# Second layer norm of a one-layer decoder: the last two experts' first-block rows become norm blocks of their own

## The chip, the cores and the metric

The kernel runs on one core of a Trainium2 chip. The metric is device time in microseconds (us) of one execution; less is better. Before the change the median of three runs is 1563.72 us (1562.43 to 1565.71). The engines are PE (TensorE, matmuls), DVE (VectorE), ACT (ScalarE), POOL (GpSimd) and SP (SyncE, which here only issues DMAs). Each engine works through its own instructions in order.

## The reference, cut to what matters

```python
def reference(x, ...):                                  # 1024 tokens, width 1024, one layer
    mix = hybrid_mixer(x, ...)                          # attention and DeltaNet branches, merged, times w_o
    x = layer_norm(ALPHA * x + mix, ln1_g, ln1_b)
    ffn = grouped_moe(x, w_router, router_bias, w_gate, w_up, w_down)
    return layer_norm(ALPHA * x + ffn, ln2_g, ln2_b)

merged = sigmoid(g_a) * (o_a @ w_br_a) + sigmoid(g_b) * (o_b @ w_br_b)     # end of hybrid_mixer
mix = merged @ w_o

# grouped_moe: each token goes to its two best experts (of 16) of one group of four
hid = silu(xb @ w_gate[e]) * (xb @ w_up[e])
ys = (hid @ w_down[e]) * row_w                          # summed per token over its two experts
```

All arrays are float32.

## The kernel before, in words

A value is split into a high and a low float32r part: ACT copies the high part (`copy`), DVE subtracts it for the low part (`lo_part`), and each product is three matmuls (`mm3`: high by high, high by low, low by high). So every weight that PE uses has passed through ACT and then DVE.

Working tiles are taken from a pool `m4` of 45 slots of 128 x 1024 (names m and l in the rows) and `m2` of 128 x 512 (h). A small model of the engines (`Clock`) only decides which free slot is taken; it puts the order of instructions in place in the first part of the kernel, and the parts that matter here are written out by hand, after `tc.manual_schedule()`. Waits between engines and DMAs follow from the tiles.

Two places of the program matter.

*Merging the branches* (`merge(d)`, eight steps, d = 0 to 7; products in tiles `pbr`). A step takes branch weights (`w_br_a`, `w_br_b`) that were split in the step before, makes four products of twelve matmuls each, and DVE multiplies each by a gate `sg`. At its start it issues on SP the loads that the next steps need: two gates (`spill`), branch weights for step d + 2, and one slab of `w_o`. In its middle it splits the branch weights of step d + 1 and the `w_o` slab; at its end ACT makes the next two gates (Sigmoid). On ACT the order over a step's border is thus: high part of the `w_o` slab of step 0, the two gates of step 1, the high part of the branch weights of step 2. DVE makes the low parts in program order between the multiplications. Right ahead of the first step, `route_consts` clears the buffers of the routing: it fills a zero tile `z` and issues on SP two stores of it (to the spare rows of `h_d` and `acc_d`) and two of initial lists (`lst`).

*Experts and second norm.* `acc_d` in HBM holds ALPHA * x per token; every expert block adds its rows by an indirect DMA (`acc_d<-m,idx`). The first block of an expert (up to 128 tokens) runs in `expert_steps` (16 steps j: eight for gate and up, products `pgu`; eight for down, `pdn`); further blocks of an expert run before it in conditional branches. The first block of expert 15 does not add its rows to `acc_d`: it gathers its rows into `lt[0]`, adds its own result, norms them as a block of their own and scatters them to the output after all others. The other rows are loaded from `acc_d` in eight blocks (`more_rows`) and normed by the generator `norm_rows`, whose pieces are put between the steps of expert 15 by the table `TAIL` (the count of pieces at each j). Per block ACT sums (Copy with accumulation) and squares (Square with accumulation), DVE forms mean, variance and two passes over the block (SCALAR_TENSOR_TENSOR), POOL takes the power -1/2 (TENSOR_TENSOR `h<-rs,mhalf`), and SP stores the block.

Of the kernel before, what the change touches and what calls it, by code (L numbers as in the profile page):

```python
# [169 lines left out]
HIGHS = 8  # L170
START = 'LLLLABHUHNLUHLUHLLUSRCLIDLLUL'
LASTF = (1, 2, 1, 0, 2, 0, 1, 0, 1, 1, 1, 1, 1, 0, 0, 0)
TAIL = (0, 0, 0, 1, 1, 0, 1, 0, 1, 0, 1, 0, 1, 1, 1, 1)
TR0 = 5
TR = 2
TURN = (2, 3, 4, 5)
# [13 lines left out]
def build(ctx, tc, x, w_in, conv_w, a_log, dt_bias, onorm_g, w_br_a, w_br_b, w_o, ln1_g, ln1_b,  # L190
# [802 lines left out]
    lst = [dp.tile([NE * S, 2], FT, name=f"lst{j}") for j in range(2)]  # L993
    h_d = dp.tile([S + JUNK, D], FT, name="h_d")
    acc_d = dp.tile([S + JUNK, D], FT, name="acc_d")
    BIG = 1.0e30
    wr = kp.tile([P, KT, NE], FT, name="wr_")
    rc = kp.tile([P, 3, NE], FT, name="rc")
# [13 lines left out]
    def route_consts():  # L1012
        Q.dma_start(wr, w_router.rearrange("(k p) e -> p k e", p=P))
        Q.dma_start(rb, view(router_bias, 0, [[0, P], [1, NE]]))
        for i, src in enumerate((ln1_g, ln1_b)):
            Q.dma_start(lnp[:, i, :], view(src, 0, [[1, P], [P, KT]]))
        G.iota(io16, pattern=[[1, NE]], base=0, channel_multiplier=0, allow_small_or_imprecise_dtypes=True)
        G.iota(ebase, pattern=[[S, NE]], base=0, channel_multiplier=0, allow_small_or_imprecise_dtypes=True)
        for j in range(2):
            G.iota(pair[:, :, j, 0], pattern=[[P, NB]], base=-S * j, channel_multiplier=1,  # L1020
                   allow_small_or_imprecise_dtypes=True)
        oh0.append(m4.get([P, 1024]))
        oh0.append(oh0[0].bitcast(BF).rearrange("p (t s) -> p t s", t=NB))
        slot0.append(m2.get([P, 512]))
        G.iota(slot0[0][:, :2 * P], pattern=[[1, 2 * P]], base=-2 * S, channel_multiplier=0, allow_small_or_imprecise_dtypes=True)
        for t in range(NB):
            V.memset(tok2[:, t, 0:1], float(P * t - S))
        G.iota(tok2[:, :, 1], pattern=[[0, NB]], base=0, channel_multiplier=1, allow_small_or_imprecise_dtypes=True)
        V.memset(ohs[:, 0, :], 0.0)
        V.memset(gs8, -BIG)  # L1030
        z = new([P, D], FT, "zero")
        V.memset(z, 0.0)
        Q.dma_start(h_d[S:, :], z)
        Q.dma_start(acc_d[S:, :], z)
        drop(z)

        for j in range(2):
            li = new([P, P, 2], FT, "linit")
            V.memset(li, 0.0)
            if j == 0:  # L1040
                V.memset(li[:, :, 0], float(S))
            Q.dma_start(lst[j].rearrange("(p s) c -> p (s c)", p=P), li.rearrange("p s c -> p (s c)"))
            drop(li)

        wk = new([P, KT + 2, NE])
        t, cs = wk[:, :KT], wk[:, KT:]
        for dst, i in ((t, 1), (wr, 0)):
            V.tensor_tensor(dst, wr, lnp[:, i, :, None].to_broadcast([P, KT, NE]), op=OP.mult)
        for i, src in enumerate((wr, t)):
            V.tensor_reduce(cs[:, i], src.rearrange("p k e -> p e k"), axis=AX.X, op=OP.add)  # L1050
        csum.append(wk)
# [551 lines left out]
    def expert_steps(e, blk, ix, wslot, tag, fill=None, pause=-1):  # L1603
# [46 lines left out]
        for j, f in enumerate(steps):  # L1650
# [10 lines left out]
            if last:  # L1661
                for _ in range(fills(e)[j]):
                    fill()
            if last and e == NE - 1:
                if j == LATE:
                    lt.append(m4.get([P, D]))
                    gather(ix, lt[0], acc_d)
                if j == 7:
                    m4.free(*xs[0])
                more_rows()  # L1670
                for _ in range(TAIL[j]):
                    next(tail, None)
        m2.free(hid, th, tl)
        if last and e == NE - 1:
            for half in range(2):
                sl = slice(512 * half, 512 * half + 512)
                V.scalar_tensor_tensor(lt[0][:, sl], py[half], wslot, lt[0][:, sl], op0=OP.mult, op1=OP.add,
                                       accum_out=lw[:, half:half + 1])
            return
        ys = m4.get([P, D])  # L1680
        for half in range(2):
# [113 lines left out]
    for blk in range(2):  # L1795
        gather(idx[:, blk, 1:2], xgs[blk])

    ts, lt, g2b2 = [], [], []
    lw = kp.tile([P, 8], FT, name="lsw")

    def more_rows():
        while len(ts) < NB and len(m4.open) > (3 if g2b2 else 5):
            tb = len(ts)
            ts.append(m4.get([P, D]))
            Q.dma_start(ts[tb], acc_d[tb * P:(tb + 1) * P, :])
            if tb == 1:
                g2b2.extend(m4.get([P, D]) for _ in range(2))
                for t, src in zip(g2b2, (ln2_g, ln2_b)):
                    Q.dma_start(t, view(src, 0, [[0, P], [1, D]]))

    def norm_rows():
        while len(m4.open) < 2:
            yield
        junk, sws = m4.get([P, D]), m2.get([P, NB, 8])
        one = two = None
        for tb in range(NB + 2):
            while len(ts) <= min(tb, NB - 1):
                yield
            cur = None
            if tb < NB:  # L1820
                cur = ts[tb], sws[:, tb, :], out[0, tb * P:(tb + 1) * P, :]
                t, sw = cur[:2]
                A.activation(junk, t, AF.Copy, accum_out=sw[:, 0:1])
                V.tensor_scalar(sw[:, 2:3], sw[:, 0:1], -1.0 / D, None, op0=OP.mult)
            elif tb == NB:
                t, sw = cur = lt[0], lw
                V.tensor_scalar(lw[:, 2:3], lw[:, 0:1], lw[:, 1:2], -1.0 / D, op0=OP.add, op1=OP.mult)
            if cur:
                A.activation(junk, t, AF.Square, bias=sw[:, 2:3], accum_out=sw[:, 3:4])
            yield  # L1830
            for early in (tb <= NB, tb > NB):
                if one and early:
                    t, sw = one[:2]
                    rsqrt_(sw[:, 4:5], sw[:, 3:4], 1, 1.0 / D, LN_EPS)
                    V.scalar_tensor_tensor(t, t, sw[:, 2:3], g2b2[0], op0=OP.add, op1=OP.mult)
                    yield
                if two and not early:
                    t, sw, dst = two
                    V.scalar_tensor_tensor(t, t, sw[:, 4:5], g2b2[1], op0=OP.mult, op1=OP.add)
                    Q.dma_start(dst, t)  # L1840
            one, two = cur, one
            yield
        m4.free(junk)

    tail = norm_rows()
    for e in range(NE):
# [35 lines left out]
                            expert_block(e, 1, li, lp[0][:, 1:2], "pb")  # L1882
        if e == NE - 1:
            m4.free(*xgs, xs[1][1])
        if e:
            begun = expert_steps(e, 0, idx[:, 0, col], wsl[:, 0, col], "pa", fill)
        if e + 1 < NE:
# [4 lines left out]
                gather(idx[:, blk, e + 2:e + 3], xgs[blk])  # L1892
    for _ in tail:
        pass
    t = lt[0]
    V.scalar_tensor_tensor(t, t, lw[:, 4:5], g2b2[1], op0=OP.mult, op1=OP.add)
    G.indirect_dma_start(out=out[0], out_offset=bass.IndirectOffsetOnAxis(ap=idx[:, 0, NE - 1:NE], axis=0),
                         in_=t, in_offset=None, bounds_check=S - 1, oob_is_err=False)


_INS = ['x', 'w_in', 'conv_w', 'a_log', 'dt_bias', 'onorm_g', 'w_br_a', 'w_br_b', 'w_o', 'ln1_g', 'ln1_b',
# [21 lines left out]
```

## Time and profile before

| | us |
|---|---|
| median of 3 runs | 1563.72 |
| the profiled execution, its own time | 1565.18 |
| its span from the first to the last instruction | 1563.4 |
| PE busy | 1433.7 (92%) |
| DVE busy | 1009.4 (65%) |
| ACT busy | 787.9 (50%) |
| POOL busy | 253.5 (16%) |

How to read the profile: a row of the timeline gives the start, the length, the engine, the instruction with output and inputs, and in brackets the idle time before it and what ended it; rows of equal instructions in a row are merged (x48), also where their tiles differ. A row with SPq is a DMA being issued: its length includes what SP waited for. A row of the table by stretches gives for each engine the busy time and the number of instructions, then the granted TensorE clock as a share of full speed (1.00 is 2.4 GHz, 0.50 is 1.2 GHz), the mean busy share of the 16 DMA engines (it can come out slightly above 1) and what they moved.

### The profile page before, as it was taken

How to read it: one execution, taken by the hardware profiler on the slowest of the kernel's cores; microseconds unless marked ns; L12 is line 12 of the kernel's file. 1: busy time of each engine (PE TensorE's matmuls, PEld its weight loads, DVE VectorE, ACT ScalarE, POOL GpSimd, SP SyncE). 2: the span in 40 equal slices, each digit the busy share in tenths (PEclk: the TensorE clock that was granted, in tenths of full speed). 3: DMA queues.
4: the chain of work that ended last, by engine and by line, in shares of the span. 5: the costliest groups of instructions: out<-in, count | busy, mean ns of one | idle time of the engine just before them, and what ended most of it. 6: DMA issues, size and time to landing. Idle time of an engine off the chain costs nothing. (4 is left out here: it accounts for less than half of the span.)

```text
span 1563.4 us, 23346 instructions
## 1 busy us (share of the span) xinstructions
PE 1433.7 (92%) x8500; PEld 1239.7 (79%) x8500; DVE 1009.4 (65%) x1829; ACT 787.9 (50%) x1491; POOL 253.5 (16%) x297
## 2 busy tenths in 40 slices
PE   7999999999999899999999999948899999899981
PEld 6888887888897779778888888647788888788871
DVE  6577746775577686877236537757487777717746
ACT  5545436543545554655343223346477665617644
POOL 0100001100111222122001002331122221112123
PEclk9999999999999999999999999979999999999995
DMA  6111222121201011025458357558589979737844
GB/s 209 42 38 42 64 58 65 38 65 55 66 17 54 27 55 35 15 67 162 141 182 304 118 180 180 197 161 270 147 264 313 302 221 307 248 83 208 291 139 198
DMA packets 185866, 219.93 MB, mean 141 GB/s; under 512 B 27604, under 2 KB 154628, under 8 KB 185696
## 3 DMA queue, kind: packets, MB, share of 16 engines
q1 hardware_dynamic: 163936, 175.61, 35.7%
q0 software_dynamic: 10048, 21.25, 5.6%
q10 hardware_dynamic: 11712, 20.98, 3.9%
q8 instruction: 86, 1.41, 0.4%
q14 instruction: 84, 0.69, 0.1%
HBM read 185.55 MB, written 45.11 MB: 148 GB/s over the span
## 5 line engine op out<-in xcount | busy, mean ns | idle before, releaser
L146 PE MATMUL pj<-m,m 128*128 128x512 f32 x1968 | 494.0, 399 | 3.8 <-ACT m L146 3.2
L146 DVE TENSOR_TENSOR m<-m,m 128x1024 fp32r<-128x1024 f32 (+9 forms) x334 | 363.8, 1107 | 143.2 <-ACT m L146 118.2
L146 PEld LDWEIGHTS pj<-m,m 128*128 128x128 f32 x1968 | 358.0, 189 | 72.3 <-ACT m L146 4.3
L146 ACT ACTIVATE m<-m 128x1024 fp32r<-128x1024 f32 (+2 forms) x308 | 313.5, 1049 | 134.7 <-DMA m<-in_w_o_dram 27.0
L146 PE MATMUL pgu<-m,m 128*128 128x256 f32 x1104 | 214.6, 287 | 8.2 <-DVE m L146 4.1
L146 PEld LDWEIGHTS pgu<-m,m 128*128 128x128 f32 x1104 | 175.6, 191 | 15.4 <-DVE m L146 6.8
L146 PE MATMUL pdn<-m,h 128*128 128x512 f32 x532 | 153.4, 419 | 16.1 <-ACT h L146 11.4
L146 PE MATMUL pgu<-m,l 128*128 128x256 f32 x512 | 143.7, 281 | 0.0
L146 PEld LDWEIGHTS pdn<-m,h 128*128 128x128 f32 x532 | 96.4, 196 | 35.9 <-ACT h L146 12.8
L146 POOL TENSOR_SCALAR_AFFINE_SELECT m<-m 128x128 f32<-128x128 f32 x128 | 66.1, 536 | 290.6 <-ACT m L146 271.2
L146 DVE TENSOR_TENSOR_SCAN m<-m 128x128 f32<-128x128 f32 (+4 forms) x64 | 88.7, 1390 | 22.4 <-POOL m L146 22.0
L146 PEld LDWEIGHTS pgu<-m,l 128*128 128x128 f32 x512 | 97.8, 191 | 0.2 <-DVE l L146 0.2
L146 PE MATMUL pgu<-m,both 128*128 128x256 f32 x572 | 87.4, 290 | 8.6 <-DVEq L1860 8.2
L146 PE MATMUL pmix<-m,m 128*128 128x512 f32 x352 | 91.8, 403 | 0.0
L146 PEld LDWEIGHTS pgu<-m,both 128*128 128x128 f32 x572 | 79.8, 195 | 10.6 <-issue 9.0
L146 ACT ACTIVATE m<-pj 64x512 fp32r<-64x512 f32 (+2 forms) x74 | 43.8, 592 | 85.4 <-PE pj L146 61.6
L146 ACT ACTIVATE m<-pz 128x512 f32<-128x512 f32 (+2 forms) x194 | 79.9, 510 | 11.6 <-PE pz L146 6.3
L146 POOL TENSOR_TENSOR rn<-rs,mhalf 128x8 f32<-128x8 f32 x12 | 28.0, 2335 | 346.2 <-DVE rs L146 346.2
L146 PE MATMUL pbr<-m,m 128*128 128x512 f32 x352 | 82.9, 390 | 0.0
L146 PEld LDWEIGHTS pmix<-m,m 128*128 128x128 f32 x352 | 66.9, 193 | 14.4
L146 PEld LDWEIGHTS pbr<-m,m 128*128 128x128 f32 x352 | 66.0, 188 | 13.8
L146 POOL DMA_INDIRECT acc_d<-m,idx x24 | 45.6, 1898 | 159.9 <-ACT m L146 44.0
(264 smaller groups left out, 2086.1 us busy)
## 6 DMA issues: line engine op xcount, KB each, us to landing
m<-in_w_down_dram SPq DMA_DIRECT2D x64, 512.0 KB
m<-in_w_gate_dram SPq DMA_DIRECT2D x58, 512.0 KB
m<-in_w_up_dram SPq DMA_DIRECT2D x54, 512.0 KB
m<-in_w_in_dram SPq DMA_DIRECT2D x45, 512.0 KB
spill<-h ACTq DMA_DIRECT2D x40, 256.0 KB
m<-spill SPq DMA_DIRECT2D x20, 512.0 KB
m<-in_x_dram SPq DMA_DIRECT2D x16, 512.0 KB
m<-in_w_o_dram SPq DMA_DIRECT2D x8, 512.0 KB
```

Source lines behind the costliest of these rows:

```text
L146: return fn(*args, **kw)
```

## The change

The first block of expert 14 is treated as that of expert 15 was: its rows are gathered from `acc_d` in the middle of its steps, get its result, and are normed as a block of their own. Its result no longer goes to `acc_d`. For tokens that have both expert 14 and expert 15 it is scattered to a second buffer `add_d`, from which expert 15's block gathers it as well and adds it. `add_d` has 1024 rows and is filled with zeros in `route_consts`, by eight stores of the tile `z`, each of 128 x 1024 float32. All eight loads of `acc_d` are issued ahead of expert 15's first step; the ln2 weights are loaded during expert 14. `norm_rows` now has ten units (expert 14's block, eight row blocks, expert 15's block). `place(0)` scatters expert 14's rows to the output after the store of the last row block, `place(1)` expert 15's rows at the end.

```diff
-TAIL = (0, 0, 0, 1, 1, 0, 1, 0, 1, 0, 1, 0, 1, 1, 1, 1)
+TAIL = (1, 2, 1, 2, 2, 1, 2, 1, 2, 1, 1, 1, 1, 1, 1, 1)
...
+    add_d = dp.tile([S, D], FT, name="add_d")
...
         Q.dma_start(h_d[S:, :], z)
         Q.dma_start(acc_d[S:, :], z)
+        for tb in range(NB):
+            Q.dma_start(add_d[tb * P:(tb + 1) * P, :], z)
         drop(z)
...
+            if last and e == NE - 2 and j == LATE:
+                lt.append(m4.get([P, D]))
+                gather(ix, lt[0], acc_d)
+                g2b2.extend(m4.get([P, D]) for _ in range(2))
+                for t, src in zip(g2b2, (ln2_g, ln2_b)):
+                    Q.dma_start(t, view(src, 0, [[0, P], [1, D]]))
             if last and e == NE - 1:
                 if j == LATE:
-                    lt.append(m4.get([P, D]))
-                    gather(ix, lt[0], acc_d)
+                    lt.extend(m4.get([P, D]) for _ in range(2))
+                    gather(ix, lt[1], acc_d)
+                    gather(ix, lt[2], add_d)
+                if j == LATE + 4:
+                    V.tensor_tensor(lt[1], lt[1], lt[2], op=OP.add)
+                    m4.free(lt[2])
...
+        if last and e == NE - 2:
+            def rest():
+                ys = m4.get([P, D])
+                for half in range(2):
+                    A.activation(ys[:, 512 * half:512 * half + 512], py[half], AF.Copy, scale=wslot)
+                with_sums(lt[0], lw[0])
+                G.indirect_dma_start(out=add_d, out_offset=bass.IndirectOffsetOnAxis(ap=ix, axis=0),
+                                     in_=ys, in_offset=None, bounds_check=S - 1, oob_is_err=False)
+                m4.free(ys)
+
+            after_more.append(rest)
             return
...
+    def place(i):
+        G.indirect_dma_start(out=out[0], out_offset=bass.IndirectOffsetOnAxis(ap=idx[:, 0, NE - 2 + i:NE - 1 + i], axis=0),
+                             in_=lt[i], in_offset=None, bounds_check=S - 1, oob_is_err=False)
...
-                    Q.dma_start(dst, t)
+                    tb = units[n - 2]
+                    if tb is not None:
+                        Q.dma_start(out[0, tb * P:(tb + 1) * P, :], t)
+                    if tb == NB - 1:
+                        place(0)
+                    if tb is None and n > 2:
+                        place(1)
...
         if e == NE - 1:
             m4.free(*xgs, xs[1][1])
+            more_rows()
+            for f in after_more:
+                f()
```

SP, ahead of the first merge step, before the change (`l_7789` is the zero tile, `m_7805` and `m_7807` the gates of step 1, `m_7809` the branch weights of step 2, `m_7812` the `w_o` slab of step 0):

```order
104 L146 DMA h_d<-l_7789 128x1024
105 L146 DMA acc_d<-l_7789 128x1024
106 L146 DMA lst_7360<-m_7793 128x256
107 L146 DMA lst_7361<-m_7797 128x256
108 L146 DMA m_7805<-spill_226 128x1024
109 L146 DMA m_7807<-spill_227 128x1024
110 L146 DMA m_7809<-in_w_br_a_dram 128x4x128
111 L146 DMA m_7809<-in_w_br_b_dram 128x4x128
112 L146 DMA m_7812<-in_w_o_dram 128x1024
```

The same place now:

```order
104 L146 DMA h_d<-l_7790 128x1024
105 L146 DMA acc_d<-l_7790 128x1024
106 L146 DMA add_d<-l_7790 128x1024 x8
107 L146 DMA lst_7360<-m_7802 128x256
108 L146 DMA lst_7361<-m_7806 128x256
109 L146 DMA m_7814<-spill_226 128x1024
110 L146 DMA m_7816<-spill_227 128x1024
111 L146 DMA m_7818<-in_w_br_a_dram 128x4x128
112 L146 DMA m_7818<-in_w_br_b_dram 128x4x128
113 L146 DMA m_7821<-in_w_o_dram 128x1024
```

The eight stores stand ahead of every load of the merge steps on SP's queue.

POOL, from the branches of expert 15 to the end, before the change (`m_24398` holds expert 15's rows, `lsw` their sums, `h_24331` those of the eight row blocks):

```order
769 L146 DMA m_24398<-acc_d,idx 128x1024
770 L146 TENSOR_TENSOR h_24331<-rs,mhalf 128x1 x8
771 L146 TENSOR_TENSOR lsw<-rs,mhalf 128x1
772 L146 DMA out_dram<-m_24398,idx 1024x1024
```

The same place now (`m_23534` and `lsw_9812` belong to expert 14's rows, `m_24437` and `lsw_9813` to expert 15's):

```order
769 L146 DMA add_d<-m_24284,idx 1024x1024
770 L146 TENSOR_TENSOR lsw_9812<-rs,mhalf 128x1
771 L146 TENSOR_TENSOR h_24309<-rs,mhalf 128x1 x2
772 L146 DMA m_24437<-acc_d,idx 128x1024
773 L146 DMA m_24438<-add_d,idx 128x1024
774 L146 TENSOR_TENSOR h_24309<-rs,mhalf 128x1 x6
775 L146 DMA out_dram<-m_23534,idx 1024x1024
776 L146 TENSOR_TENSOR lsw_9813<-rs,mhalf 128x1
777 L146 DMA out_dram<-m_24437,idx 1024x1024
```

The scatter of expert 14's rows now stands ahead of the power for expert 15's rows, and the gather of expert 15's rows behind the powers of the first blocks.

## Rows read from the trace of the kernel before

**Rows 1.** The page, part 1: busy time of each engine, its share of the span, and its instructions.

```profile
PE 1433.7 (92%) x8500; PEld 1239.7 (79%) x8500; DVE 1009.4 (65%) x1829; ACT 787.9 (50%) x1491; POOL 253.5 (16%) x297
```

**Rows 2.** The table by stretches around the first merge steps: stretch and its length, busy time (and instructions) of PE, PEld, DVE, ACT, POOL, then granted clock, DMA share, GB/s.

```profile
790.00:800.00 10.00, 10.00 (x46) 8.29 (x45) 3.58 (x3) 3.53 (x5) 0.00 (x0) 1.00 0.11 42
800.00:805.00 5.00, 5.00 (x24) 4.14 (x23) 3.54 (x14) 2.43 (x3) 0.00 (x0) 1.00 0.14 52
805.00:810.00 5.00, 5.00 (x23) 4.14 (x23) 2.40 (x8) 3.14 (x4) 0.00 (x0) 1.00 0.90 319
810.00:815.00 5.00, 5.00 (x23) 4.14 (x23) 1.82 (x2) 0.00 (x0) 0.00 (x0) 1.00 1.01 338
...
830.00:835.00 5.00, 5.00 (x23) 4.13 (x22) 3.04 (x5) 3.91 (x4) 0.00 (x0) 1.00 1.07 382
835.00:840.00 5.00, 5.00 (x23) 4.10 (x22) 2.67 (x5) 2.75 (x3) 1.08 (x2) 1.00 0.46 133
```

**Rows 3.** The timeline of SP ahead of and in the first merge step.

```profile
804.92 0.34 SPq L146 DMA_DIRECT2D h_d<-l  x1
805.30 0.43 SPq L146 DMA_DIRECT2D acc_d<-l  x1
805.83 2.09 SPq L146 DMA_DIRECT2D lst<-m  x2
808.02 1.40 SPq L146 DMA_DIRECT2D m<-spill  x2
...
810.57 0.48 SPq L146 DMA_DIRECT2D m<-in_w_o_dram  x1
```

**Rows 4.** The timeline of ACT: four instructions from the high part of the first `w_o` slab to the high part of step 2's branch weights, and the same of the next step.

```profile
817.22 3.91 ACT L146 ACTIVATE m<-m 128x1024 fp32r<-128x1024 f32 x4 [8.65 <-DMA m<-in_w_o_dram]
823.82 2.96 ACT L146 ACTIVATE m<-m 128x1024 fp32r<-128x1024 f32 x3 [2.69 <-DMA m<-in_w_o_dram]
```

**Rows 5.** The timeline of DVE: from the low part of the first `w_o` slab (first row) to the low part of step 2's branch weights (last row).

```profile
818.31 1.23 DVE L146 TENSOR_TENSOR m<-m,m 128x1024 fp32r<-128x1024 f32 x1 [6.47 <-ACT m L146]
...
822.21 1.27 DVE L146 TENSOR_TENSOR m<-m,pbr 128x512 f32<-128x512 f32 x2
823.40 1.22 DVE L146 TENSOR_TENSOR m<-m,m 128x1024 fp32r<-128x1024 f32 x1
```

**Rows 6.** The timeline of PE in the merge steps: step 0 (48 matmuls), then steps 1 and 2 (96).

```profile
804.38 11.04 PE L146 MATMUL pbr<-m,m 128*128 128x512 f32 x48
815.26 0.30 PE L146 MATMUL pcs<-m,ones 128*128 128x32 f32 x2
815.40 22.06 PE L146 MATMUL pbr<-m,m 128*128 128x512 f32 x96
```

**Rows 7.** The DMA view of 812 to 830 us (first row) and of 1531 to 1552 us, where the eight output blocks are stored (the other two rows; the last is that of the queue with its share of the 16 engines' time).

```profile
DMA packets 4617, 6.82 MB, mean 379 GB/s; under 512 B 270, under 2 KB 3342, under 8 KB 4614
DMA packets 1301, 4.75 MB, mean 226 GB/s; under 512 B 141, under 2 KB 141, under 8 KB 1301
q1 hardware_dynamic: 1301, 4.75, 55.2%
```

**Rows 8.** The table by stretches of 6 us that begin where PE resumes after an idle time of 3 to 5.5 us (columns as in rows 2).

```profile
1058.90:1064.90 6.00, 5.62 (x20) 4.01 (x21) 5.69 (x8) 4.19 (x8) 0.00 (x0) 0.66 1.06 386
1108.20:1114.20 6.00, 5.99 (x28) 6.00 (x29) 0.00 (x0) 0.00 (x0) 4.34 (x4) 0.51 0.87 177
1185.60:1191.60 6.00, 5.95 (x28) 5.18 (x29) 3.66 (x5) 3.33 (x6) 0.80 (x2) 0.72 1.00 344
1369.60:1375.60 6.00, 5.99 (x38) 6.00 (x39) 0.00 (x0) 0.00 (x0) 4.35 (x4) 0.72 0.87 189
1497.70:1503.70 6.00, 5.66 (x16) 4.13 (x17) 5.44 (x8) 3.50 (x6) 0.00 (x0) 0.54 0.08 33
```

**Rows 9.** Timelines at the border of experts 14 and 15: PE's last six matmuls of expert 14, ACT's scaling of its result, DVE's last low part, the scatter of its rows, SP's first two loads of `acc_d`, and ACT's first block sum.

```profile
1507.68 1.63 PE L146 MATMUL pdn<-m,h 128*128 128x512 f32 x6
1509.35 0.69 ACT L146 ACTIVATE m<-pdn,wsl 128x512 f32<-128x512 f32 x1 [0.20 <-PE pdn L146]
1510.01 0.68 DVE L146 TENSOR_TENSOR l<-pxe,m 128x512 fp32r<-128x512 f32 x1
1510.32 1.63 POOL L146 DMA_INDIRECT acc_d<-m,idx  x1 [1.71 <-ACTq L1858]
1516.73 0.80 SPq L146 DMA_DIRECT2D m<-acc_d  x2
1520.32 1.06 ACT L146 ACTIVATE m<-m 128x1024 f32<-128x1024 f32 x1 [4.49 <-DMA m<-acc_d]
```

**Rows 10.** The timeline of DVE in the second norm: one of the four small steps of expert 15 (first row), the sums of its block (one half), the mean of two row blocks that follow each other, and the last passes.

```profile
1523.23 0.42 DVE L146 TENSOR_TENSOR h<-phd,h 128x256 fp32r<-128x256 f32 x1 [1.58 <-ACT h L146]
...
1531.64 0.75 DVE L146 SCALAR_TENSOR_TENSOR m<-pdn,wsl,m 128x512 f32<-128x512 f32 x1
...
1538.08 0.15 DVE L146 TENSOR_SCALAR h<-h 128x1 f32<-128x1 f32 x1
...
1540.72 0.15 DVE L146 TENSOR_SCALAR h<-h 128x1 f32<-128x1 f32 x1
...
1546.07 3.67 DVE L146 SCALAR_TENSOR_TENSOR m<-m,h,m 128x1024 f32<-128x1024 f32 x3
...
1551.43 1.28 DVE L146 SCALAR_TENSOR_TENSOR m<-m,lsw,m 128x1024 f32<-128x1024 f32 x1 [0.44 <-POOL lsw L146]
```

**Rows 11.** The table by stretches: the middle of expert 14's steps to their end, and the stretch of the second norm in which PE has ended (columns as in rows 2).

```profile
1496.00:1509.50 13.50, 10.65 (x43) 7.74 (x43) 11.79 (x14) 10.80 (x17) 1.73 (x2) 0.75 0.14 45
1531.00:1548.00 17.00, 0.00 (x0) 0.00 (x0) 16.84 (x29) 12.54 (x22) 9.09 (x6) 0.59 0.53 216
```

**Rows 12.** One step near the end of the chain that ended last: the store of the last row block, from its issue to its landing (start, us).

```profile
1549.76 3.08 DMA out_dram<-m
```

**Rows 13.** The timeline of POOL at the end: the power for expert 15's rows and the scatter of its rows to the output.

```profile
1549.87 1.52 POOL L146 TENSOR_TENSOR lsw<-rs,mhalf 128x1 f32<-128x1 f32 x1 [2.13 <-DVE rs L146]
1553.95 1.05 POOL L146 DMA_INDIRECT out_dram<-m,idx  x1 [2.56 <-issue]
```

More of the change, by code (lines that the diff above doesn't have):

```diff
@@ L1673, in expert_steps, with with_sums @@
         m2.free(hid, th, tl)
-        if last and e == NE - 1:
+        def with_sums(t, sums):
             for half in range(2):
                 sl = slice(512 * half, 512 * half + 512)
-                V.scalar_tensor_tensor(lt[0][:, sl], py[half], wslot, lt[0][:, sl], op0=OP.mult, op1=OP.add,
-                                       accum_out=lw[:, half:half + 1])
+                V.scalar_tensor_tensor(t[:, sl], py[half], wslot, t[:, sl], op0=OP.mult, op1=OP.add,
+                                       accum_out=sums[:, half:half + 1])
+        if last and e == NE - 1:
+            with_sums(lt[1], lw[1])
+            return
+        if last and e == NE - 2:
[8 more added lines that the diff above has]
+            after_more.append(rest)
             return
@@ L1796, in build @@
         gather(idx[:, blk, 1:2], xgs[blk])
-    ts, lt, g2b2 = [], [], []
-    lw = kp.tile([P, 8], FT, name="lsw")
+    ts, lt, g2b2, after_more = [], [], [], []
+    lw = [kp.tile([P, 8], FT, name=f"lsw{i}") for i in range(2)]
     def more_rows():
-        while len(ts) < NB and len(m4.open) > (3 if g2b2 else 5):
+        while len(ts) < NB and len(m4.open) > 4:
             tb = len(ts)
@@ L1805, in more_rows @@
             Q.dma_start(ts[tb], acc_d[tb * P:(tb + 1) * P, :])
[L1806 to L1809, printed above, removed]
+    def place(i):
+        G.indirect_dma_start(out=out[0], out_offset=bass.IndirectOffsetOnAxis(ap=idx[:, 0, NE - 2 + i:NE - 1 + i], axis=0),
+                             in_=lt[i], in_offset=None, bounds_check=S - 1, oob_is_err=False)
     def norm_rows():
@@ L1814, in norm_rows @@
         junk, sws = m4.get([P, D]), m2.get([P, NB, 8])
+        units = [None] + list(range(NB)) + [None]
         one = two = None
-        for tb in range(NB + 2):
-            while len(ts) <= min(tb, NB - 1):
-                yield
[L1819 to L1831, printed above, removed]
+        for n in range(NB + 4):
+            cur = None
+            if n < NB + 2:
+                tb = units[n]
+                if tb is None:
+                    i = int(n > 0)
+                    t, sw = cur = lt[i], lw[i]
+                    V.tensor_scalar(sw[:, 2:3], sw[:, 0:1], sw[:, 1:2], -1.0 / D, op0=OP.add, op1=OP.mult)
+                else:
+                    while len(ts) <= tb:
+                        yield
+                    t, sw = cur = ts[tb], sws[:, tb, :]
+                    A.activation(junk, t, AF.Copy, accum_out=sw[:, 0:1])
+                    V.tensor_scalar(sw[:, 2:3], sw[:, 0:1], -1.0 / D, None, op0=OP.mult)
+                A.activation(junk, t, AF.Square, bias=sw[:, 2:3], accum_out=sw[:, 3:4])
+                yield
+            for early in ((True, False) if n <= NB + 1 else (False, True)):
                 if one and early:
-                    t, sw = one[:2]
+                    t, sw = one
                     rsqrt_(sw[:, 4:5], sw[:, 3:4], 1, 1.0 / D, LN_EPS)
@@ L1837, in norm_rows @@
                 if two and not early:
-                    t, sw, dst = two
+                    t, sw = two
                     V.scalar_tensor_tensor(t, t, sw[:, 4:5], g2b2[1], op0=OP.mult, op1=OP.add)
-                    Q.dma_start(dst, t)
+                    tb = units[n - 2]
[5 more added lines that the diff above has]
+                        place(1)
             one, two = cur, one
@@ L1894, in build @@
         pass
[L1895 to L1898, printed above, removed]
 _INS = ['x', 'w_in', 'conv_w', 'a_log', 'dt_bias', 'onorm_g', 'w_br_a', 'w_br_b', 'w_o', 'ln1_g', 'ln1_b',
```

## The prediction, made before the result was known

> **What bounds the kernel now.** I read the page first. Its busy times [rows 1] put PE in front with 1433.7 of 1563.4 us, so time is lost or won where PE waits or has already ended. The change touches two such places, and I read the table by stretches and the timelines of both.
>
> The first is the start of the merge steps. Up to 805 us the DMA engines are nearly idle (shares of 0.11 and 0.14), from 805 to 835 us they are full (0.90 to 1.07, 319 to 382 GB/s), and after 835 us half idle again, while PE is busy in every microsecond [rows 2]. SP issues two stores of zeros, two of lists, and then the loads of the merge steps one behind the other [rows 3]. ACT stands idle for 8.65 us until the first `w_o` slab has landed at 817.2, and only then makes the gates of step 1 and the high part of step 2's branch weights, ended at 817.22 + 3.91 = 821.1 [rows 4]. DVE follows from 818.31 without a gap and ends the low part of those weights at 823.40 + 1.22 = 824.6 [rows 5]. PE's 96 matmuls of steps 1 and 2 take 22.06 us from 815.40 [rows 6], so step 2 begins at 815.40 + 11.03 = 826.4, and its third matmul, the first that needs the low part, at 826.4 + 2 x 0.23 = 826.9. So PE runs without a break, but the cover is thin: 826.9 - 824.6 = 2.3 us between the low part and its use, and the whole chain hangs on a landing in a full queue.
>
> The second place is the end. Expert 14's last matmul ends at 1507.68 + 1.63 = 1509.3, its rows are scattered from 1510.32, the loads of `acc_d` go out at 1516.73, and ACT begins the norm at 1520.32 after an idle time of 4.49 us [rows 9]. From 1531 us on DVE is the bound of the norm, with 16.84 of 17 us busy [rows 11]; a row block costs it 1540.72 - 1538.08 = 2.64 us [rows 10]. The last passes of the row blocks end at 1546.07 + 3.67 = 1549.7 [rows 10], the last store lands 3.08 us after its issue [rows 12], and the scatter of expert 15's rows, which waits for it, starts at 1553.95 [rows 13]; 9.4 us later the span ends.
>
> **The change part by part.** *The eight stores of zeros.* They move 8 x 128 x 1024 x 4 bytes = 4.19 MB and stand on SP's queue ahead of all loads of the merge steps. At the rate of the full stretch, 379 GB/s, they take 11.1 us; at that of the output stores, which are stores of the same shape (4.75 MB in 0.552 x 21 = 11.6 us of full use, 410 GB/s), 10.2 us [rows 7]. The nearest slower row, 338 GB/s [rows 2], gives 12.4 us, the upper bound. I take 10.7 us, between the first two. Nothing hides it: the zero tile is ready just before 804.92, where the first store of it goes out [rows 3], so the idle queue before that can't be used, and the queue behind it is full at once. Each of the loads lands 10.7 us later, the first `w_o` slab at 817.2 + 10.7 = 827.9, and the low part of step 2's weights, 824.6 - 817.2 = 7.4 us behind it through ACT and DVE, at 835.3. PE wants it at 826.9: it loses 835.3 - 826.9 = 8.4 us (bounds 10.2 - 2.3 = 7.9 and 12.4 - 2.3 = 10.1). The high part comes at 821.1 + 10.7 = 831.8, so PE is idle from 826.4 for 5.4 us, does two matmuls, and is idle for another 3 us.
>
> After idle times of 3 to 5.5 us this trace shows PE at the lower of its two clock levels for a while: in the 6 us behind five such gaps the mean granted clock was 0.66, 0.51, 0.72, 0.72 and 0.54 [rows 8]. On a stream of matmuls that costs (1 - clock) x 6 = 2.0, 2.9, 1.7, 1.7 and 2.8 us, on average 2.2 us, which I add; the bounds are 1.7 and 2.9.
>
> Does the wait repeat at the next step? The second `w_o` slab would land at 823.8 + 10.7 = 834.5 and ACT's four instructions after it end by 838.4; the low part of step 3's weights comes behind DVE's first two multiplications of step 2, which PE sets; with step 2 running from 835 us at first at half clock, that is some 846 us, and step 3 wants it at 826.4 + 8.4 + 2.2 + 11.0 + 0.5 = 848.5. So once is enough, with 2.5 us to spare. From there to the experts' end PE is in front, and loads wait for slots that PE and DVE free, so I take the whole 8.4 + 2.2 = 10.6 us as a shift of everything behind.
>
> In the page "DMA: Bandwidth & Descriptors", section Specifications, the Trainium skill gives an HBM limit of about 358 GB/s per core; by it the stores would take an estimated 4.19 / 0.358 = 11.7 us and the sum would be 1.0 us higher. The trace shows 379 GB/s over 18 us [rows 7], so the sum goes by the row.
>
> *Loads and gathers in expert 14's steps.* The gather, the two ln2 loads and the earlier loads of `acc_d` fall into 1496 to 1516 us, where the DMA engines are at 0.14 [rows 11] and SP has nothing else to issue. No instruction of expert 14 waits for them. Cost 0; if their cover were gone (a late slot), the first norm block would be late, which the next part holds in its bounds. The loads need no scatter of expert 14 any more, only slots, the last of which its final matmuls free at 1509.3; with 1520.32 - 1516.73 = 3.6 us to landing [rows 9] the first, issued at about 1504, is there long before ACT comes to it at 1513.7.
>
> *The norm's start.* ACT scales expert 14's result twice (0.69 each [rows 9]) and ends at 1510.7; DVE is free at 1510.01 + 0.68 = 1510.7 and sums the two halves by 1512.2 (0.75 each [rows 10]); ACT squares that block and sums the first row block, for which I take one block's pace, 2.64 us, so DVE's steady work begins at 1514.8. That work to the end of the last row block is nine blocks x 2.64 = 23.8, the sums of expert 15's block 1.5, the added addition of two 128 x 1024 tiles 1.2 (as the low parts of rows 5), four small steps of expert 15 of 0.4, 1.6 [rows 10]: together 28.1; I add 1.3 for one wait on a pass of ACT (1.06 [rows 9] and its signals) in the first blocks. It ends at 1544.2, against 1549.7: 5.5 us won, one block more and all.
>
> *The end.* POOL scatters expert 14's rows only when the last store has landed, and the power for expert 15's rows now stands behind that scatter on POOL. Before, power and last pass lay under the landing. Now, behind 1544.2: to the scatter's start 1553.95 - 1549.74 = 4.2; the scatter 1.05; the power 1.52 and 0.1 of signals [rows 13]; the last pass 1.28 [rows 10]; and 0.6 until the second scatter starts. That is 1553.0, against 1553.95: of the 5.5 us 0.9 are left. The price of the order alone is 8.8 - 4.2 = 4.6 us. So this part counts as -0.9, with the bounds -4.0 (two thirds of the 4.6 not paid) and +0.9 (the gather from `add_d` comes behind three powers on POOL at about 1523 us; if it landed 1.8 us after DVE wants it, DVE's addition would wait so long).
>
> **Sum.** 8.4 + 2.2 - 0.9 = 9.7 us over the profiled execution: 1565.18 + 9.7 = 1574.9. That execution is 1.46 us above the median of the runs, so against the median 1563.72 + 9.7 = 1573.4.
>
> **The rivals.** A: the stores cost nothing, because PE's cover holds (the queue serves loads beside them). Then only the end counts: 1563.72 - 0.9 = 1562.8, no change. For it: the 2.3 us of cover and the empty queue before 805. Against: the queue is at 1.01 or above for 20 us behind [rows 2], and the loads are issued later on the same queue.
>
> B, the other side: the stores are hidden, and the power does not wait behind the scatter long enough to matter, so the norm's earlier start arrives in full: 1563.72 - 5.5 = 1558.2, faster. It decides from the point at which POOL reaches the power before the last store has landed; POOL's order speaks against it.
>
> C: half. If stores and loads overlapped so that the stores delay the slab by 5.4 us, PE would lose 5.4 - 2.3 = 3.1, and 1.7 of clock: 3.1 + 1.7 - 0.9 = 3.9, 1567.6. The row of 830 to 835 us speaks against: at a share of 1.07 the engines move 382 GB/s and no more [rows 2].
>
> D: the wait repeats at step 3, with the 2.5 us of spare eaten by a slower stretch. If a whole 8.4 us came again, 1581.8; half of it, 1577.6.
>
> **How the numbers follow.** Forecast 0.73, A 0.06, B 0.05, C 0.08, D 0.08. The forecast's own bounds are 7.9 + 1.7 - 4.0 = 5.6 and 10.1 + 2.9 + 0.9 = 13.9, that is 1569.3 to 1577.6. To hold 8 in 10 the range takes in C and half of D: 1567.5 to 1580. 0.2% is 3.1 us, about what a measurement of this kernel can tell from no change: B is faster, with 0.01 of A (0.06); the rest of A and 0.01 of C are the same (0.06); all else is slower (0.88).
>
> **What would show it.** In the changed kernel's profile: the DMA share full from 805 to about 846 us instead of 835; ACT's idle time ahead of the first `w_o` slab near 19 us instead of 8.65; PE, unbroken so far, idle for some 5 and 3 us at the start of the merge products' third step, with the clock at 0.50 behind; all later stages about 10.6 us late. At the end the norm's first square some 7 us nearer to expert 14's end than before, the store of the last row block 5 us earlier beside PE's end, and POOL with a scatter between the seventh block's power and the last one. The prediction is wrong if PE shows no idle time at 826 us, or if the shift is gone before the experts begin.

## The result, and the profile after

The changed kernel takes 1575.74 us (median of 6 runs, 1573.01 to 1577.78) where the kernel before takes 1563.72 on the same chip: a ratio of 1.0074, 95% interval 1.0061 to 1.0088. The medians lie 12.0 us apart, and the interval goes from 9.5 to 13.8 us. The prediction had 9.7 us and 1573.4. The profiled execution, 1574.94 us with a span of 1573.2, is 9.8 us longer than that of before, in span and in time.

**The start of the merge steps.** First SP's timeline, the counterpart of [rows 3]:

```profile
805.33 0.43 SPq L146 DMA_DIRECT2D acc_d<-l  x1
805.81 9.70 SPq L146 DMA_DIRECT2D add_d<-l  x8
815.61 2.98 SPq L146 DMA_DIRECT2D lst<-m  x2
818.69 0.96 SPq L146 DMA_DIRECT2D m<-spill  x2
...
820.79 0.60 SPq L146 DMA_DIRECT2D m<-in_w_o_dram  x1
```

The eight stores stand where the lists stood, and the load of the first `w_o` slab is issued at 820.79 instead of 810.57. ACT's timeline ([rows 4]):

```profile
827.59 3.90 ACT L146 ACTIVATE m<-m 128x1024 fp32r<-128x1024 f32 x4 [19.00 <-DMA m<-in_w_o_dram]
833.24 2.95 ACT L146 ACTIVATE m<-m 128x1024 fp32r<-128x1024 f32 x3 [1.75 <-DMA m<-in_w_o_dram]
```

The number in brackets has grown from 8.65 to 19.00 us: the slab lands 10.4 us later. PE's timeline ([rows 6]):

```profile
815.44 11.14 PE L146 MATMUL pbr<-m,m 128*128 128x512 f32 x48
831.54 1.22 PE L146 MATMUL pbr<-m,m 128*128 128x512 f32 x2 [4.96 <-ACT m L146]
835.04 15.24 PE L146 MATMUL pbr<-m,m 128*128 128x512 f32 x60 [2.28 <-DVE m L146]
```

What was one unbroken row of 96 matmuls is now 48, a wait for ACT's high part, two matmuls, a wait for DVE's low part. The two matmuls take 1.22 us where such a pair took 0.46. The table by stretches ([rows 2]; clock, DMA share and GB/s are the last three columns) shows both causes:

```profile
810.00:815.00 5.00, 5.00 (x24) 4.15 (x23) 1.82 (x2) 0.00 (x0) 0.00 (x0) 1.00 1.03 419
...
825.00:830.00 5.00, 1.58 (x7) 0.96 (x6) 1.32 (x2) 2.41 (x3) 0.00 (x0) 1.00 1.04 375
830.00:835.00 5.00, 1.22 (x2) 0.50 (x2) 4.93 (x9) 3.25 (x4) 1.36 (x2) 0.61 1.06 381
835.00:840.00 5.00, 4.96 (x16) 3.98 (x17) 4.39 (x6) 2.18 (x4) 1.08 (x2) 0.71 1.07 388
840.00:845.00 5.00, 5.00 (x24) 4.14 (x23) 3.29 (x4) 3.87 (x4) 0.00 (x0) 1.00 1.06 386
845.00:850.00 5.00, 5.00 (x24) 4.14 (x23) 2.39 (x5) 3.42 (x4) 1.08 (x2) 1.00 0.55 162
```

The DMA engines are full for some 10 us longer than before, to about 845 (by stretches of 1 us the share is 0.34 from 845 to 846 and 0.00 after it; before it fell to 0.25 from 835 to 836). PE, idle for 7.2 us in all, comes back at a granted clock of 0.61 and 0.71 in two stretches: 16 matmuls in a stretch that holds 24.

**The end.** PE's last six matmuls of expert 14, ACT's first square of the norm, and the last passes of the row blocks on DVE ([rows 9, 10]), from three timelines:

```profile
1518.51 1.63 PE L146 MATMUL pdn<-m,h 128*128 128x512 f32 x6
```

```profile
1523.49 1.15 ACT L146 ACTIVATE m<-m,lsw 128x1024 f32<-128x1024 f32 x1 [2.05 <-issue]
```

```profile
1551.92 3.67 DVE L146 SCALAR_TENSOR_TENSOR m<-m,h,m 128x1024 f32<-128x1024 f32 x3
...
1561.10 1.29 DVE L146 SCALAR_TENSOR_TENSOR m<-m,lsw,m 128x1024 f32<-128x1024 f32 x1 [4.26 <-POOL lsw L146]
```

The norm starts 1523.49 - 1520.14 = 3.4 us behind expert 14's last matmul, before it was 11.0 (to the first block sum, which stood first then). From the start of the six matmuls to the end of the last row block's pass it takes 1555.59 - 1518.51 = 37.1 us; before, 1549.74 - 1507.68 = 42.1. So 5.0 us are won there. POOL's timeline ([rows 13]) shows where they go:

```profile
1552.08 1.52 POOL L146 TENSOR_TENSOR h<-rs,mhalf 128x1 f32<-128x1 f32 x1 [1.06 <-DVE rs L146]
1559.42 1.04 POOL L146 DMA_INDIRECT out_dram<-m,idx  x1 [5.83 <-issue]
1560.50 0.57 POOL L146 TENSOR_TENSOR lsw<-rs,mhalf 128x1 f32<-128x1 f32 x1
1563.51 1.04 POOL L146 DMA_INDIRECT out_dram<-m,idx  x1 [2.44 <-DMA out_dram<-m,idx]
```

From the six matmuls to the last scatter: 1563.51 - 1518.51 = 45.0 us, before 1553.95 - 1507.68 = 46.3. Only 1.3 us are left. What ended POOL's last wait is not the power or DVE, but the landing of the first scatter. The chain that ended last says the same (start, us, what):

```profile
1555.61 2.74 DMA out_dram<-m
...
1559.42 3.29 DMA out_dram<-m,idx
```

One landing behind the other, where [rows 12] had one.

### The profile page after: what moved, and what is told of

It is laid out like the page before. It is cut to its first block, busy times and chain, and to the rows that moved or that the text cites. A ratio compares the mean times of both kernels' runs of the same rounds, so it can differ in the third digit from the quotient of the medians.

```text
span 1573.2 us, 23378 instructions
## 1 busy us (share of the span) xinstructions
PE 1438.9 (91%) x8500; PEld 1243.1 (79%) x8500; DVE 1014.4 (64%) x1838; ACT 788.8 (50%) x1493; POOL 257.2 (16%) x301
## 5 line engine op out<-in xcount | busy, mean ns | idle before, releaser
L146 DVE TENSOR_TENSOR m<-m,m 128x1024 fp32r<-128x1024 f32 (+8 forms) x319 | 347.1, 1105 | 152.9 <-ACT m L146 128.2
L146 ACT ACTIVATE m<-m 128x1024 fp32r<-128x1024 f32 (+2 forms) x299 | 304.6, 1049 | 136.5 <-DMA m<-in_w_o_dram 26.3
L146 PE MATMUL pgu<-m,m 128*128 128x256 f32 x1564 | 221.5, 287 | 8.3 <-DVE m L146 4.2
L146 PEld LDWEIGHTS pgu<-m,m 128*128 128x128 f32 x1564 | 203.6, 194 | 15.7 <-DVE m L146 12.5
L146 PEld LDWEIGHTS pdn<-m,h 128*128 128x128 f32 x512 | 94.0, 198 | 32.7 <-ACT h L146 10.4
L146 PE MATMUL pbr<-m,m 128*128 128x512 f32 x384 | 89.9, 395 | 7.2 <-ACT m L146 5.0
L146 PEld LDWEIGHTS pbr<-m,m 128*128 128x128 f32 x384 | 73.0, 191 | 23.5 <-ACT m L146 5.4
L146 PEld LDWEIGHTS pgu<-m,both 128*128 128x128 f32 x560 | 77.6, 193 | 10.6 <-issue 9.0
L146 PE MATMUL po<-h,m 128*128 128x256 f32 x320 | 55.6, 290 | 16.3 <-DVE h L146 15.1
L146 PEld LDWEIGHTS po<-h,m 128*128 128x128 f32 x320 | 47.2, 192 | 25.7 <-DVE h L146 20.8
```

Source lines behind the costliest of these rows:

```text
L146: return fn(*args, **kw)
```

## The experiments

The times of one kernel differ by several us from run to run, so next to the timed ratio I read two lengths from each trace that the two changed places alone set: the **merge length**, from the small matmul `pcs` ([rows 6]) to the first `pmix` matmul, and the **tail length**, from the start of expert 14's last six `pdn` matmuls to the start of the last scatter. Before: 891.93 - 815.26 = 76.7 and 46.3 us. "PE idle" is the sum of the waits in PE's timeline in the merge; "clock" is what the merge length has grown by beyond that; it includes what the pair of matmuls between the two waits lost. The edits are described below the table.

| kernel | ratio to before (95%) | merge length, growth | PE idle | clock | tail length |
|---|---|---|---|---|---|
| changed | 1.0074 (1.0061 to 1.0088) | 86.05, +9.4 | 7.2 | 2.1 | 45.0 |
| changed, again | 1.0066 (1.0043 to 1.0089) | 87.46, +10.8 | 7.3 | 3.5 | 45.0 |
| rows | 0.9980 (0.9971 to 0.9990) | 76.64, 0.0 | 0 | 0 | 45.0 |
| rows, again | 0.9983 (0.9974 to 0.9992) | 76.64, 0.0 | 0 | 0 | 45.0 |
| before + 4 stores | 1.0030 (1.0018 to 1.0041) | 81.75, +5.1 | 3.2 | 1.9 | 46.0 |
| before + 8 stores | 1.0086 (1.0066 to 1.0106) | 87.27, +10.6 | 8.4 | 2.2 | 46.3 |
| before + 16 stores | 1.0154 (1.0133 to 1.0174) | 98.10, +21.4 | 19.0 | 2.4 | 46.2 |
| stores on POOL's queue | 1.0066 (1.0050 to 1.0081) | 86.84, +10.2 | 7.9 | 2.3 | 45.0 |
| place order | 1.0073 (1.0044 to 1.0103) | 87.29, +10.6 | 7.2 | 3.4 | 45.0 |
| one scatter | 1.0050 (1.0030 to 1.0070) | 86.00, +9.3 | 7.1 | 2.2 | 40.9 |
| rows, addition on POOL | 0.9999 (0.9990 to 1.0008) | 76.64, 0.0 | 0 | 0 | 45.7 |

**Without the eight stores (rows).** Theory: the stores cost everything. Rival: the new gathers and the second scatter do.

```diff
-    add_d = dp.tile([S, D], FT, name="add_d")
...
-        for tb in range(NB):
-            Q.dma_start(add_d[tb * P:(tb + 1) * P, :], z)
...
+    add_d = mg_d.rearrange("k p s -> (k p) s")
...
     for blk in range(2):
         gather(idx[:, blk, 1:2], xgs[blk])
+    G.indirect_dma_start(out=add_d, out_offset=bass.IndirectOffsetOnAxis(ap=idx[:, 0, NE - 1:NE], axis=0),
+                         in_=xgs[2], in_offset=None, bounds_check=S - 1, oob_is_err=False)
```

> The changed kernel, without the eight zero stores at the start of the merge: in their place one scatter of zero rows (512 KB), issued by POOL ahead of the first expert, clears just the rows that expert 15's tokens gather; the buffer lies in the memory of the merge's result, which is dead by then. Theory 'the stores cost it all': the first w_o slab lands near 817 again, PE has no idle stretch of 5 us at the third merge step, and what is left of the change is the tail, 0.9 to 1.5 us ahead: 1562 to 1563 us, a ratio to before of 0.9985 to 0.9997. Rival 'the tail pays' (gathers, second scatter, loads behind expert 14): the time stays within 3 us of the changed kernel's 1575.7, so above 1572. Rival 'both': 1566 to 1571.

Measured: 1560.84 us against 1563.17 of before on that chip, ratio 0.9980. PE has no wait in the merge and its length is that of before to 0.03 us; the tail is 45.0. ACT's and PE's timelines, the counterparts of [rows 4, 6]:

```profile
814.90 3.91 ACT L146 ACTIVATE m<-m 128x1024 fp32r<-128x1024 f32 x4 [8.48 <-DMA m<-in_w_o_dram]
```

```profile
813.25 22.03 PE L146 MATMUL pbr<-m,m 128*128 128x512 f32 x96
```

The loss is gone with the stores, and the rest of the change is a gain. This edit writes an eighth of the bytes, and writes them at another place, on POOL and ahead of the first expert; which of the two would do by itself was not tried. The rivals fall, though the time is a microsecond below the range of the theory too. Run a second time:

> The kernel of the row scatter once more, beside its variant: 0.9 to 2.5 us ahead of before, a ratio of 0.9984 to 0.9994; the stretch from the start of expert 14's last six down products to the last scatter 45.0 us.

1561.89 against 1564.22, ratio 0.9983, the same two lengths. The two traces of this one kernel have spans of 1557.0 and 1562.6 us; so 5.6 us lie between two executions outside both places, and this is why a single time says little here. The timed gain of 2.3 us is larger than the 1.3 us that the tail shows; the second interval holds 1.3, the first ends just short of it, and where another microsecond comes from stays open.

**The stores alone, in three doses.** Added to the kernel before, into a buffer that nothing reads; n is 4, 8 or 16:

```diff
+    add_d = dp.tile([S, D], FT, name="add_d")
...
         Q.dma_start(acc_d[S:, :], z)
+        for tb in range(n):
+            Q.dma_start(add_d[tb % NB * P:(tb % NB + 1) * P, :], z)
```

> The kernel before, with nothing added but the eight zero stores of 512 KB to a buffer that nothing reads. Theory 'the stores cost it all': 8.4 us of wait and 2.2 us of lower clock behind it, 10.6 in all, so 1574.3 us (1573 to 1576), no tail gain taken off. Rival 'the tail pays': 1562.5 to 1565, no change.

> The kernel before with four zero stores of 512 KB instead of eight. If the weights wait out each store and the merge has some 2.3 us of slack ahead of them, as the prediction's sum has it (5.3 us later, 2.3 of it hidden): 3.0 us of wait and 0 to 2.2 us of clock, so 1566.7 to 1569. If there is no slack and cost goes with bytes: half of eight's, 5 to 6 us, 1569 to 1570. If a few stores fit into idle DMA time: 1564 or less.

> The kernel before with sixteen zero stores of 512 KB (each of the buffer's eight blocks twice). By the prediction's sum, 10.7 us for eight stores and 2.3 us of slack: 21.4 - 2.3 + 2.2 of clock = 21.3 us, so 1584 to 1586. By the line through what four and eight stores measured (3.9 and 11.2 us, 7.3 for four): 3.9 + 3 x 7.3 = 25.8 us, 1589.

Measured: 1574.36, 1567.05 and 1585.14 us; beside the before runs on each chip +11.2, +3.9 and +24.6. Eight stores alone make the whole loss. PE's waits, first and second, in the timelines with 4, 8 and 16 stores:

```profile
825.08 0.73 PE L146 MATMUL pbr<-m,m 128*128 128x512 f32 x2 [0.40 <-ACT m L146]
828.57 21.61 PE L146 MATMUL pbr<-m,m 128*128 128x512 f32 x87 [2.76 <-DVE m L146]
```

```profile
831.85 1.22 PE L146 MATMUL pbr<-m,m 128*128 128x512 f32 x2 [6.11 <-ACT m L146]
835.35 14.84 PE L146 MATMUL pbr<-m,m 128*128 128x512 f32 x58 [2.28 <-DVE m L146]
```

```profile
842.77 1.22 PE L146 MATMUL pbr<-m,m 128*128 128x512 f32 x2 [16.74 <-ACT m L146]
846.27 59.02 PE L146 MATMUL pbr<-m,m 128*128 128x512 f32 x252 [2.27 <-DVE m L146]
```

With 4 stores PE is idle for 3.2 us, with 8 for 8.4, with 16 for 19.0: 1.3 us a store between 4 and 16, and the line through these meets zero at 4 - 3.2 / 1.3 = 1.6 stores, 2.1 us. That is the cover of the prediction, 2.3 us, seen from outside.

The growth of the merge length alone, 5.1, 10.6 and 21.4 us, would not tell this cover from the second expectation's rival, no slack and a cost that goes with the bytes: it is about 1.3 us a store throughout, because what the cover hides and what the clock adds nearly cancel. The timelines do tell them apart. ACT's, with 4, 8 and 16 stores:

```profile
821.12 3.90 ACT L146 ACTIVATE m<-m 128x1024 fp32r<-128x1024 f32 x4 [14.44 <-DMA m<-in_w_o_dram]
```

```profile
827.90 3.90 ACT L146 ACTIVATE m<-m 128x1024 fp32r<-128x1024 f32 x4 [20.17 <-DMA m<-in_w_o_dram]
```

```profile
838.83 3.90 ACT L146 ACTIVATE m<-m 128x1024 fp32r<-128x1024 f32 x4 [30.80 <-DMA m<-in_w_o_dram]
```

Counted from each trace's own `pcs` (813.38, 814.43 and 814.73), the slab lands 5.8, 11.5 and 22.1 us later than before, and step 2's third matmul starts 3.6, 9.3 and 19.9 us late: 2.2 us less each time. The eight stores delay the slab by 11.5 us here and by 10.3 in the changed kernel; no run tells why.

The clock term is 1.9, 2.2 and 2.4 us, one trace each, so it hardly grows while the wait grows sixfold; the five traces with eight stores on SP's queue alone spread from 2.1 to 3.5 us. In the merge length 16 stores cost 21.4 us, where the prediction's sum has 21.3 and the straight line through the timed values of 4 and 8 has 25.8. The timed +24.6 can't tell the two apart, since its interval goes from 20.8 to 27.2; the trace can.

**The same stores on another queue.** Does the place in SP's queue cost the time, or do the bytes?

```diff
-            Q.dma_start(add_d[tb * P:(tb + 1) * P, :], z)
+            G.dma_start(add_d[tb * P:(tb + 1) * P, :], z)
```

> The changed kernel with the same eight zero stores issued by POOL on its own queue, so that SP's loads stand behind nothing. Theory 'bytes': both queues are served by the same 16 DMA engines, which are full at this stretch, so the loads are late by as many bytes as go beside them: 1571 to 1576. Rival 'place in SP's queue': the loads keep their time, 1562 to 1565.

Measured: 1572.40 us, +9.2. SP issues its first loads at 805.43 now, none of the eight stores ahead of them, and yet (ACT's timeline, then the DMA view from 803 to 826 us with each queue's share of the 16 engines' time):

```profile
825.57 3.90 ACT L146 ACTIVATE m<-m 128x1024 fp32r<-128x1024 f32 x4 [19.66 <-DMA m<-in_w_o_dram]
```

```profile
DMA packets 3589, 8.76 MB, mean 381 GB/s; under 512 B 303, under 2 KB 1583, under 8 KB 3587
...
q1 hardware_dynamic: 2291, 4.28, 49.5%
q0 software_dynamic: 1152, 4.19, 49.3%
```

The two queues share the engines half and half, and the slab is 825.57 - 812.62 = 12.95 us behind `pcs`, before it was 1.96: 11.0 us late, about as with the stores ahead of it (10.3 and 11.5). This is what the Trainium skill's page "DMA: Bandwidth & Descriptors", section Issuing engines are not separate DMA queues, states: DMAs of any issuing engine end up on the same 16 engines and interleave there. The trace agrees.

**The order at the end.** The prediction put the lost part of the tail down to POOL's order, the power for expert 15 behind the first scatter. The trace after names another reason, the landing of the first scatter. Two kernels tell them apart. One moves the scatter behind the power, the other leaves it out, each from the changed kernel, which ran once more beside them:

```diff
-                    if tb == NB - 1:
-                        place(0)
                     if tb is None and n > 2:
+                        place(0)
                         place(1)
```

```diff
-                    if tb == NB - 1:
-                        place(0)
```

> The changed kernel once more, as the measure of the two beside it: 1573 to 1578 us.

> The changed kernel with the scatter of expert 14's rows moved behind the power of expert 15's rows in POOL's order, both scatters then one after the other. The prediction priced that order at 4.6 us, so by it the end comes 2 to 4.6 us sooner than in the changed kernel beside it (1571 to 1573.5). New theory: the second scatter waits for the landing of the first (both write the output), and the first for the last row block's store, so the order costs nothing: the second scatter still goes out some 7.9 us behind the end of the last row block's second pass, and the time is that of the changed kernel within 1 us.

> The changed kernel with the scatter of expert 14's normed rows left out (those rows of the output keep what the row blocks stored, without expert 14's part). New theory: the remaining scatter then goes out right behind the last store's landing or expert 15's second pass, some 3.9 to 4.1 us behind the end of the last row block's pass in place of 7.9: 3.8 to 4.1 us sooner than the changed kernel. Rival (the end hangs on DVE's work, not on the scatters): less than 1 us sooner.

Measured: the changed kernel 1571.87 us, below what was expected, as before is on this chip with 1560.55 (the ratio, 1.0066, agrees with the first one); the other order 1573.43, 1.6 us slower than the changed kernel instead of within 1; without the first scatter 1568.04, 3.8 sooner. The intervals of all three overlap, so it is the traces that decide. POOL's timeline with the other order, and then without the scatter:

```profile
1554.24 1.51 POOL L146 TENSOR_TENSOR lsw<-rs,mhalf 128x1 f32<-128x1 f32 x1 [2.13 <-DVE rs L146]
1557.92 1.04 POOL L146 DMA_INDIRECT out_dram<-m,idx  x1 [2.17 <-issue]
1561.99 0.98 POOL L146 DMA_INDIRECT out_dram<-m,idx  x1 [3.03 <-DMA out_dram<-m,idx]
```

```profile
1549.99 1.51 POOL L146 TENSOR_TENSOR lsw<-rs,mhalf 128x1 f32<-128x1 f32 x1 [2.13 <-DVE rs L146]
1553.69 1.05 POOL L146 DMA_INDIRECT out_dram<-m,idx  x1 [2.18 <-DVE m L146]
```

With the power early, expert 15's rows are ready long before they can go: the second scatter still waits for the first one's landing, and the tail is 45.0 us to 0.01 us as before the edit. So beside that landing the order costs nothing. The two waits lie over each other: in the changed kernel the last pass ends at 1561.10 + 1.29 = 1562.39, and with the 0.87 us that the kernel without the first scatter takes from there to its scatter (1552.82 to 1553.69), the order alone would have let the second scatter go at an estimated 1563.3, against the 1563.51 at which the landing did. No run takes away the landing alone. Without the scatter the tail is 1553.69 - 1512.76 = 40.9 us, and from the end of the last row block's pass to the last scatter it is 3.8 us instead of 7.9: the scatter costs 4.1.

**DVE's work on another engine.** From the kernel of the row scatter, in search of a faster one:

```diff
-                    V.tensor_tensor(lt[1], lt[1], lt[2], op=OP.add)
+                    G.tensor_tensor(lt[1], lt[1], lt[2], op=OP.add)
```

> The row scatter's kernel, with the sum of expert 15's two gathered rows (one 128x1024 add, 1.22 us on DVE) moved from DVE to POOL. If DVE's steady work sets the last row block's end, the end comes 1.0 to 1.2 us sooner: 43.8 to 44.0 us from expert 14's last six down products to the last scatter. Rival: POOL's add stands in front of the powers, each of which DVE waits for in turn, or slows DVE while both run: no gain, or up to 2 us longer.

Measured: 1563.95 us, ratio to before 0.9999 (0.9990 to 1.0008), where the row scatter's kernel beside it has 0.9983. The tail is 1551.17 - 1505.47 = 45.7 us. POOL's and DVE's timelines:

```profile
1528.19 2.66 POOL L146 TENSOR_TENSOR m<-m,m 128x1024 f32<-128x1024 f32 x1 [0.36 <-DMA m<-mg_d,idx]
1530.83 1.51 POOL L146 TENSOR_TENSOR h<-rs,mhalf 128x1 f32<-128x1 f32 x1
```

```profile
1526.15 2.47 DVE L146 SCALAR_TENSOR_TENSOR m<-m,h,m 128x1024 f32<-128x1024 f32 x2
...
1528.66 4.48 DVE L146 SCALAR_TENSOR_TENSOR m<-m,h,m 128x1024 f32<-128x1024 f32 x2
```

While POOL adds, a pair of passes takes DVE 4.48 us instead of 2.47: of the 1.2 us taken off DVE, 2.0 come back. The Trainium skill's page "SBUF — State Buffer", section SBUF: two separate sides, says that DVE and GpSimd share one pair of ports, that a DVE instruction with two inputs in SBUF contends for it with a GpSimd instruction that reads SBUF (both are so here), that the first to start has it for its whole instruction, and that the other is blocked. By that DVE, begun at 1528.66 behind POOL's 1528.19, would stand until POOL's end at 1530.85 and then need 2.47, an estimate of 4.66 us against the 4.48 in the trace, which so agrees.

## Why the prediction was right, point by point

- *What bounds the kernel:* right in the main. Both places decided; what else answers to the change stands under "all later stages".
- *The eight stores, 10.7 us:* right. The slab is 10.4 us later here and 10.3 with the start of both traces set equal (`pcs` 0.04 us apart); in the kernel before with the same eight stores it is 11.5 later, inside the bounds of 10.2 and 12.4.
- *The wait, 8.4 us:* nearly. PE was idle for 4.96 and 2.28 us (predicted 5.4 and 3), 7.2 in all, and the pair between took 0.76 us more at the lower clock; so step 2's third matmul started at 835.04 instead of 815.44 + 11.03 + 0.46 = 826.9, 8.1 us late. The low part came 835.04 - 827.59 = 7.45 us behind the slab, as reckoned (7.4). The cover of 2.3 us is confirmed by the doses, 2.2 in each.
- *The clock, 2.2 us:* there, but too large as the sum uses it. The sum adds 2.2 (1.7 to 2.9) behind the late start of the third matmul. Behind it 9.4 - 8.1 = 1.3 us were lost in the profiled execution, 1.3 to 1.5 in six of the eight traces with a wait, below the lower bound, and 2.5 and 2.7 in the other two. The "clock" column shows 1.9 to 2.4 in the same six (3.4 and 3.5 in the others) because it counts the pair too, and what the pair lost lay inside the wait, at no cost of its own. Both together make 9.4 us in the profiled execution, 9.3 to 10.8 in the four others with the eight stores on SP's queue, against 10.6.
- *No repeat at step 3:* right; PE's row from 835.04 on has no wait.
- *"All later stages about 10.6 us late":* true as a sum, not for each stage, and "I take the whole 8.4 + 2.2 = 10.6 us as a shift of everything behind" is a step that does not hold. In the profiled execution expert 14's end is 10.83 us late, but the merge gives 9.4 of it. In the routing stage (first `pmix` to the experts' first `pxe`) 1.9 us came back, in the experts 3.3 were lost, at the same instructions. The clock did most of the first: before, two stretches of 10 us stand at 0.84, after, one at 0.83, which is 3.2 - 1.7 = 1.5 us of PE's work (table by stretches from 930 to 950 us before, and from 930 to 960 after, where the same work lies 9.4 us later):

```profile
930.00:940.00 10.00, 10.00 (x44) 8.39 (x45) 6.50 (x46) 3.52 (x7) 1.51 (x1) 0.84 0.30 97
940.00:950.00 10.00, 9.89 (x52) 8.28 (x51) 8.54 (x39) 4.47 (x8) 0.00 (x0) 0.84 0.32 111
```

```profile
930.00:940.00 10.00, 10.00 (x68) 9.02 (x66) 2.26 (x7) 2.79 (x6) 0.00 (x0) 1.00 0.11 23
940.00:950.00 10.00, 10.00 (x41) 8.09 (x40) 7.79 (x46) 3.52 (x7) 1.52 (x1) 0.83 0.29 93
950.00:960.00 10.00, 9.89 (x59) 8.38 (x58) 8.24 (x45) 5.35 (x9) 1.09 (x1) 1.00 0.38 126
```

  This is more than spread: the routing stage takes 129.7 to 131.4 us in all eight traces with a wait in the merge and 131.7 to 132.4 in the four without; the means are 2.0 us apart. What makes the clock fall for less long there was not tried.

  In the experts PE was busy for 439.3 us instead of 435.7 with the same 3000 matmuls, so the 3.3 us lie in PE's pace and not in a wait. Whether they belong to the change stays open: the stage takes 483.6 to 487.5 us in the eight traces with a wait and 480.7 to 483.9 in the four without, and the row scatter's kernel alone has 480.7 in one execution and 483.9 in the other.
- *The sum, 9.7 us:* in part luck. The two places alone make 9.4 - 1.3 = 8.1 us of the 9.8 by which the profiled execution is longer, and the rest is what the later stages lost and gave back. The timed +12.0 (9.5 to 13.8) holds 9.7 but not 8.1; the second measurement, +11.3 (6.7 to 13.9), holds both.
- *Loads and gathers in expert 14's steps, cost 0:* right in cost, wrong in time. The first load of `acc_d` was to go out at about 1504; it went at 1520.91, which is 1510.1 once the shift of 10.83 is taken off. The step that failed is "only slots, the last of which its final matmuls free": in the trace all eight loads went out one behind the other from 1520.91 on, so none found a slot before expert 14's end. That is where DVE ended the low part of a 128 x 1024 tile (1519.70 + 1.21 = 1520.91), and in all eight traces with the change the first load goes out within 0.2 us of the end of that low part; this points to the slot that it frees, but it was not tried. ACT came to the first row block at 1524.77, when it had landed.
- *The norm's start, 5.5 us:* 5.0 measured. Less the shift of 10.83, the first square began at 1512.7, where 1512.2 was reckoned, and the last row block's pass ended at 1544.8 instead of 1544.2.
- *The end, -0.9:* -1.3 measured, and here the mechanism was half of it and the sum came out by luck. The step "the price of the order alone is 8.8 - 4.2 = 4.6 us" named POOL's order and left out the first scatter's landing. The runs show that taking the order away gains nothing, and that a second scatter to the output, which waits until the first has landed, costs 4.1. The sum came out because both waits end within an estimated 0.2 us of each other. The bound of -4.0 ("two thirds of the 4.6 not paid") was out of reach by the one reordering that was tried.
- *The rivals:* A and C fall with the doses and with the stores on POOL's queue, where "the queue serves loads beside them" was tried to the letter. B's faster end exists for neither order. D's second wait is in no trace, not even with 16 stores.

## What to carry to other kernels

Before bytes are added to a queue, look at what the DMA engines do behind that place and how much cover the next load has: here 4 MB of zeros, written 700 us before they were needed, stood in a stretch where PE lives on the loads just landed, and cost 1.3 us per 512 KB once 2.3 us of cover were spent, plus 1.9 to 3.5 us of lower clock. Moving them to another queue at the same place changed nothing; clearing just the 128 rows that are read, and at a later place, turned a loss of 0.7% into a gain of 0.2%. And count the landings in a row at the end of a kernel: here a second scatter to the same tensor cost its issue and a full landing, 4.1 us, however early its data were ready.

## What was not expected of the hardware

The clock's price was nearly the same for a wait of 3.2 us as for one of 19.0 (1.9 and 2.4 us, one trace each), and a wait in the merge gave about 2 us back in the routing stage behind it. And one kernel's two profiled executions differed by 5.6 us in span with the same instructions and no change in the two places that had been edited, which is four times what the change's own gain in the tail amounts to.
